# Gate and up products of a feed-forward as 2x2 block products: seven quarter products instead of eight

## The chip, the cores and the metric

The kernel runs on one core of one Trainium2 chip. The metric is the device time of one execution, in microseconds. Three runs of the kernel before took 3021.64 to 3022.8 us, median 3022.2. The engines are called TensorE (PE in the profile's rows), VectorE (DVE), ScalarE (ACT), GpSimd (POOL) and SyncE (SP), whose queue here starts the loads of weights.

## What is computed

Two encoder layers over 512 tokens of width 1024, all in float32. Cut to its skeleton, the reference is:

```python
def swiglu(x, w_gate, w_up, w_down):
    return (jax.nn.silu(x @ w_gate) * (x @ w_up)) @ w_down
...
for i in range(DEPTH):
    h = h + 0.5 * swiglu(rms_norm(h, ffn1_norm[i]), ffn1_w_gate[i], ffn1_w_up[i], ffn1_w_down[i])
    u = rms_norm(h, mix_norm[i])
    proj = u @ w_in[i]
    ...
    h = h + merged @ w_out[i]
    h = h + 0.5 * swiglu(rms_norm(h, ffn2_norm[i]), ffn2_w_gate[i], ffn2_w_up[i], ffn2_w_down[i])
    gate = jax.nn.sigmoid(rms_norm(h, ple_norm[i]) @ ple_w_gate[i])
    h = h + gate * (p[i] @ ple_w_proj[i])
return rms_norm(h, final_norm)
```

`w_gate` and `w_up` are 1024 x 2816, `w_down` is 2816 x 1024. `merged` is the gated sum of three attentions, which the change does not touch.

## The kernel before, in words

**Layout.** The stream `h` lies on chip as eight tiles of 128 features x 512 tokens. A product computes 128 output features x 512 tokens in one PSUM bank. To keep float32 accuracy, each operand is split into a rounded high part and the rest (`hi`, `lo`), and every product is three matmuls: high by high, low by high, high by low (`mm3`, whose matmuls the profile gives as L165). One column tile of gate or up takes 8 x 3 = 24 matmuls of 512 columns.

**Weights.** All weights come as 456 chunks of 128 x 1024 (512 KB), in the order of use, through SyncE's queue (`Weights.load`, four buffers `wraw`). `Weights.halve` splits a chunk: ScalarE casts the high part (L75), VectorE subtracts for the low part (L76; in the mixes GpSimd does that, by `lo_engine`). `get` keeps the splits two chunks ahead of the products and the loads five.

**Feed-forward** (`ffn`, called for FFN1 and FFN2 of each layer, `ffn10`, `ffn20`, `ffn11`, `ffn21` in the profile). Its right operand `z` (named `f_0z`, `f_1z`) is h times the norm's gain, split, made per tile of h by `Prep.split` (ScalarE L328, VectorE L329) while the stage before ends; the reciprocal root of the mean square is multiplied in later, and the squares are added up on GpSimd (L287). For each of 22 column tiles `f`: gate, up, then VectorE multiplies both by the root (L386, L388), ScalarE applies Silu (L387), VectorE multiplies (L389) and the result is split (L175, L176). After the tiles of a group (2, 4, 4, 4, 4, 4) its down products follow, whose sums VectorE adds to h (L371).

**Around it.** A mix ends with the output projection (`w_out`, `add_out`): the first four tiles of h are summed while the last attention heads still run; the other four come after them, all four at once, chunk after chunk over the rows. Then VectorE adds each sum to h (L944) and calls the preparation for FFN2. `ple` multiplies in the layer embedding: per tile a gate product, a tanh on ScalarE, three operations on VectorE (L972, L974, L975), then the preparation of the next layer's FFN1.

**Order.** Each engine runs its queue in order. A scheduler places the instructions by their priority in the program and by what they wait for; the order on record of each engine is what is compared below. `S` gives one of `SLOTS` = 79 buffers of 128 x 512; `PS` gives one of eight PSUM banks.

Of the kernel before, what the change touches and what calls it, by code (L numbers as in the profile page):

```python
# [45 lines left out]
class Weights:  # L46
# [21 lines left out]
    def halve(self, upto):  # L68
        while self.split < min(upto, self.total):
            n = self.split  # L70
            self.load(n + 1)
            raw = self.raw.pop(n)
            hi = self.pool.tile([P, 1024], F32R, tag="whi", name=f"whi{n}", bufs=3)
            lo = self.pool.tile([P, 1024], F32R, tag="wlo", name=f"wlo{n}", bufs=3)
            self.nc.scalar.copy(hi, raw)  # L75
            self.lo_engine.tensor_tensor(lo, raw, hi.bitcast(F32), op=ALU.subtract)  # L76
# [60 lines left out]
def encoder_kernel(ctx: ExitStack, tc: tile.TileContext, ins, out):  # L137
# [8 lines left out]
    W = Weights(nc, wpool, ins["wall"])  # L146

# [206 lines left out]
    def ffn(l, tag, prep, after, hooks={}):  # L354
        name = f"{tag}{l}"
        z = prep.z
        a = {}
        rb = None

        def down(g, final=False):  # L360
            fs = GROUPS[g]
# [13 lines left out]
        for f in range(FT):
            pg, pu = PS(f"{name}g{f}"), PS(f"{name}u{f}")
            gate, up = ("cols", tag + "_w_gate", l, f), ("cols", tag + "_w_up", l, f)
            if f == 0:
                together((pg, pu), W.get(gate, up), z)
                rb, emit = prep.norm.rstd()  # L380
                emit()
            else:
                run(proj(pg, W.get(gate), z))
                run(proj(pu, W.get(up), z))
            g1, u1 = S(f"{name}g1_{f}"), S(f"{name}u1_{f}")
            nc.vector.tensor_mul(g1, pg, rb)  # L386
            nc.scalar.activation(g1, g1, AF.Silu)  # L387
            nc.vector.tensor_mul(u1, pu, rb)  # L388
            nc.vector.tensor_mul(u1, u1, g1)  # L389
            a[f] = split(u1, f"{name}a{f}")  # L390
            for g, fs in enumerate(GROUPS[:-2]):
                if f == fs[-1] + 1:
                    down(g)
            if f in hooks:
                hooks[f]()
        root_table()
        down(len(GROUPS) - 2)
# [782 lines left out]
```

## Time and profile before

| | |
|---|---|
| median of three runs | 3022.2 us |
| the profiled execution | 3021.5 us |
| its span in the trace | 3019.7 us |
| first FFN1 / its mix / its FFN2 (us from the span's start) | 9.7 to 375.5 / 375.5 to 1103.2 / 1103.2 to 1463.1 |
| layer embedding, layer 0 | 1463.1 to 1507.5 |
| second FFN1 / its mix / its FFN2 | 1507.5 to 1868.5 / 1868.5 to 2598.2 / 2598.2 to 2958.2 |
| VectorE in a FFN2 of 360 us | 184 us busy |
| GpSimd in a FFN2 of 360 us | 15 us busy |

A row of the timeline gives the start, the duration, the engine, the line, the operation, its tile and operands, its shape, and in brackets the idle time before it and who ended it. A recorded duration holds some overlap with the next instruction, so the step from start to start is the price in a full queue.

### The profile page before, as it was taken

What the parts mean: (1) busy time and instruction counts of PE and PEld (TensorE: products, weight loads), DVE (VectorE), ACT (ScalarE), POOL (GpSimd) and SP (SyncE); (2) the same over time, 40 slices, a digit from 0 to 9 for tenths busy, and PEclk for the clock granted to TensorE, in tenths of its full rate; (3) what the DMA queues carried; (4) which work ended last, traced back from release to release, by engine and by line L of the source; (5) the groups of instructions that cost most, each with busy time, mean ns of one, the idle gap of its engine ahead of it and who ended that gap; (6) DMA issues with size and microseconds to landing.
All of it is one profiled execution on the core that took longest, in us unless ns stands there. A gap on an engine that the chain in (4) does not pass through costs nothing.

```text
span 3019.7 us, 37502 instructions
## 1 busy us (share of the span) xinstructions
PE 2966.6 (98%) x14206; PEld 2463.6 (82%) x14206; DVE 1837.0 (61%) x2844; ACT 1418.5 (47%) x2511; POOL 749.0 (25%) x709
## 2 busy tenths in 40 slices
PE   8999999999999999999999999999999999999998
PEld 7888878888878888888888888788888788888886
DVE  6444576646787765444664445866478877644446
ACT  4222356655677742223432223566467777422233
POOL 0010015444455530000200001144344555200003
PEclk9999999999999999999999999999999999999999
DMA  4363332122222233333333334211222222333332
GB/s 154 99 221 98 122 126 70 49 70 73 77 77 79 76 116 98 97 93 97 125 103 95 96 98 158 83 63 57 63 82 74 68 75 75 124 95 96 98 98 91
DMA packets 81525, 287.75 MB, mean 95 GB/s; under 512 B 10382, under 2 KB 12430, under 8 KB 81344
## 3 DMA queue, kind: packets, MB, share of 16 engines
q1 hardware_dynamic: 66960, 240.42, 25.5%
q0 software_dynamic: 12080, 42.00, 4.1%
q10 hardware_dynamic: 2304, 2.94, 0.3%
q8 instruction: 111, 1.82, 0.2%
q14 instruction: 70, 0.57, 0.1%
HBM read 274.76 MB, written 18.94 MB: 97 GB/s over the span
## 4 chain that ended last, share of the span: by engine, by line
PE 88%; DVE 6%; ACT 4%; issue 2%; POOL 0%; DMA 0%; ACTq 0%; DVEq 0%; POOLq 0%
PE ffn10g L165 4%; PE ffn10u L165 4%; PE ffn21g L165 4%; PE ffn20g L165 4%; PE ffn21u L165 4%; PE ffn20u L165 4%; PE ffn21d L165 4%; PE ffn11d L165 4%; PE ffn10d L165 4%; PE ffn20d L165 4%; PE ffn11g L165 4%; PE ffn11u L165 4%; PE wo L165 3%; PE ple L165 3%; PE m1ga L165 1%
## 5 line engine op out<-in xcount | busy, mean ns | idle before, releaser
L75 ACT CAST whi<-wraw 128x1024 fp32r<-128x1024 f32 x456 | 478.4, 1052 | 1057.0 <-issue 371.3
L76 DVE TENSOR_TENSOR wlo<-wraw,whi 128x1024 fp32r<-128x1024 f32 x312 | 383.6, 1232 | 124.3 <-ACT whi L75 124.0
L76 POOL TENSOR_TENSOR wlo<-wraw,whi 128x1024 fp32r<-128x1024 f32 x144 | 353.4, 2457 | 366.5 <-ACT whi L75 322.0
L287 POOL TENSOR_TENSOR pg0sq<-pg0sq,pg0sq 128x512 f32<-128x512 f32 x7 | 11.1, 1586 | 345.0 <-ACT pg0sq L282 345.0
L287 POOL TENSOR_TENSOR pg1sq<-pg1sq,pg1sq 128x512 f32<-128x512 f32 x7 | 11.1, 1583 | 345.1 <-ACT pg1sq L282 345.1
L419 POOL DMA_DIRECT2D h_dram<-wo0h x8 | 4.3, 541 | 341.2 <-DVE wo0h L371 341.2
L371 DVE SCALAR_TENSOR_TENSOR wo0h<-ffn11d,wo0h 128x512 f32<-128x512 f32 x48 | 32.8, 689 | 40.9 <-PE ffn11d L165 40.9
L371 DVE SCALAR_TENSOR_TENSOR x<-ffn10d,x 128x512 f32<-128x512 f32 x48 | 32.8, 689 | 40.9 <-PE ffn10d L165 40.9
L371 DVE SCALAR_TENSOR_TENSOR wo1h<-ffn21d,wo1h 128x512 f32<-128x512 f32 x48 | 32.8, 689 | 38.7 <-PE ffn21d L165 38.7
L371 DVE SCALAR_TENSOR_TENSOR wo0h<-ffn20d,wo0h 128x512 f32<-128x512 f32 x48 | 32.8, 689 | 38.7 <-PE ffn20d L165 38.7
L388 DVE TENSOR_TENSOR ffn20u<-ffn20u,f_0r 128x512 f32<-128x512 f32 x22 | 15.2, 691 | 62.0 <-PE ffn20u L165 62.0
L388 DVE TENSOR_TENSOR ffn21u<-ffn21u,f_1r 128x512 f32<-128x512 f32 x22 | 15.2, 691 | 62.0 <-PE ffn21u L165 62.0
L388 DVE TENSOR_TENSOR ffn10u<-ffn10u,f_0r 128x512 f32<-128x512 f32 x22 | 15.2, 691 | 59.8 <-PE ffn10u L165 59.8
L419 POOL DMA_DIRECT2D h_dram<-x x8 | 4.3, 540 | 189.1 <-DVE x L371 189.1
L388 DVE TENSOR_TENSOR ffn11u<-ffn11u,f_1r 128x512 f32<-128x512 f32 x22 | 15.2, 691 | 59.2 <-PE ffn11u L165 59.2
L386 DVE TENSOR_TENSOR ffn21g<-ffn21g,f_1r 128x512 f32<-128x512 f32 x22 | 15.2, 691 | 47.0 <-PE ffn21g L165 46.9
L386 DVE TENSOR_TENSOR ffn20g<-ffn20g,f_0r 128x512 f32<-128x512 f32 x22 | 15.2, 691 | 47.0 <-PE ffn20g L165 46.9
L386 DVE TENSOR_TENSOR ffn10g<-ffn10g,f_0r 128x512 f32<-128x512 f32 x22 | 15.2, 691 | 44.5 <-PE ffn10g L165 44.4
L386 DVE TENSOR_TENSOR ffn11g<-ffn11g,f_1r 128x512 f32<-128x512 f32 x22 | 15.2, 690 | 44.1 <-PE ffn11g L165 44.1
L248 POOL DMA_DIRECT2D bias_s<-bvs x1 | 0.5, 519 | 142.5 <-DVE bvs L246 142.5
L287 POOL TENSOR_TENSOR f_1sq<-f_1sq,f_1sq 128x512 f32<-128x512 f32 x14 | 21.0, 1500 | 58.5 <-ACT f_1sq L282 58.3
L598 ACT CAST m0kc<-m0kc 64x512 fp32r<-64x512 f32 x32 | 18.6, 580 | 13.7 <-PE m0kc L165 6.1
(5072 smaller groups left out, 10383.7 us busy)
## 6 DMA issues: line engine op xcount, KB each, us to landing
wraw<-in_wall SPq DMA_DIRECT2D x456, 512.0 KB, 3.5
copies_s<-bias_s POOLq DMA_DIRECT2D x16, 256.0 KB, 7.7
copies_d<-bias_d POOLq DMA_DIRECT2D x8, 512.0 KB, 15.1
h_dram<-x POOLq DMA_DIRECT2D x8, 256.0 KB, 2.7
pp_dram<-m0ppt POOLq DMA_DIRECT2D x8, 256.0 KB, 4.7
wo0h<-h_dram POOLq DMA_DIRECT2D x8, 256.0 KB, 5.3
ple0p<-pp_dram POOLq DMA_DIRECT2D x8, 256.0 KB, 4.9
h_dram<-wo0h POOLq DMA_DIRECT2D x8, 256.0 KB, 2.7
```

The lines of the kernel that those rows point to most:

```text
L75: self.nc.scalar.copy(hi, raw)
L76: self.lo_engine.tensor_tensor(lo, raw, hi.bitcast(F32), op=ALU.subtract)
L165: nc.tensor.matmul(ps, lhsT, rhs, start=start, stop=stop, skip_group_check=True)
L248: nc.gpsimd.dma_start(bias_s, bv[0:n, :])
L287: self.engine.tensor_tensor(self.acc, self.acc, sq, op=ALU.add)
L371: nc.vector.scalar_tensor_tensor(h[d], ps, 0.5, h[d], op0=ALU.mult, op1=ALU.add)
L386: nc.vector.tensor_mul(g1, pg, rb)
L388: nc.vector.tensor_mul(u1, pu, rb)
L419: nc.gpsimd.dma_start(h_dram[d], h[d])
L598: nc.scalar.copy(ks[e][r], ps[own])
```

## The change

Gate and up are computed for pairs of column tiles. The chunks of the two tiles are called `X` and `Y`; the left half of each holds the tile's first 512 rows, the right half the other 512. The 512 tokens are cut into halves `A` and `B` of 256. So a pair is a product of 2x2 blocks, for which Winograd's form of Strassen's scheme needs seven block products, four additions of weights, four of right operands and seven of results, instead of eight products. A block product is 4 x 3 = 12 matmuls of 256 columns (line L228 now), and a pair of tiles takes 84 of these instead of 48 of 512. There are 86 such blocks; layer 0's first pair of FFN1 is computed as before (`plain_pair`). In the order on record, matmuls of 512 columns go from 11334 to 7206, of 256 from 1458 to 8682; two-tensor operations of 512 on VectorE from 733 to 1179 and on GpSimd from 67 to 497.

The sums of weights stand on GpSimd (`Quad.add`), the additions of results on ScalarE (copies), VectorE and, one of them, GpSimd. The weights are split by halves of a chunk. The right operands come from `Combos` in place of `Prep`:

```diff
+        def operands(self, d):
+            name, k, gain = self.name, d % 4, col(self.l, self.at + d)
+            A, B = HALVES
+            if d < 4:
+                zf = S(f"{name}zf{d}")
+                nc.scalar.activation(zf, h[d], AF.Copy, scale=gain)
...
+                hi, lo = [t[:, HALVES[d % 2]] for t in self.both]
+                nc.scalar.copy(hi, zf[:, A])
+                nc.vector.tensor_sub(lo, zf[:, A], hi.bitcast(F32))
+                self.pair(1, k, hi, lo)
+                t = S(f"{name}t13{k}")
+                nc.vector.tensor_sub(t[:, A], zf[:, B], zf[:, A])
+                th, tl = S(f"{name}t13{k}h", F32R), S(f"{name}t13{k}l", F32R)
+                nc.scalar.copy(th[:, A], t[:, A])
+                nc.vector.tensor_sub(tl[:, A], t[:, A], th[:, A].bitcast(F32))
+                self.pair(5, k, th[:, A], tl[:, A])
...
+            else:
+                zf, t, th, tl = self.first[k]
...
+                nc.scalar.activation(hi, h[d], AF.Copy, scale=gain)
+                w = S(f"{name}t24{k}")
+                nc.vector.scalar_tensor_tensor(w[:, A], h[d][:, B], gain, t[:, A], op0=ALU.mult, op1=ALU.subtract)
+                nc.vector.scalar_tensor_tensor(w[:, B], h[d][:, A], gain, w[:, A], op0=ALU.mult, op1=ALU.subtract)
+                nc.vector.scalar_tensor_tensor(t[:, B], h[d][:, B], gain, zf[:, B], op0=ALU.mult, op1=ALU.subtract)
+                nc.vector.scalar_tensor_tensor(lo, h[d], gain, hi.bitcast(F32), op0=ALU.mult, op1=ALU.subtract)
...
+                nc.scalar.copy(wh, w)
+                nc.vector.tensor_sub(wl, w, wh.bitcast(F32))
...
+                nc.scalar.copy(th[:, B], t[:, B])
+                nc.vector.tensor_sub(tl[:, B], t[:, B], th[:, B].bitcast(F32))
...
+    class Quad:
+        def add(self):
+            X, Y = [W.raw[n] for n in self.places]
...
+            nc.gpsimd.tensor_tensor(s12[:, L], Y[:, L], Y[:, R], op=ALU.add)
+            nc.gpsimd.tensor_tensor(s12[:, R], s12[:, L], X[:, L], op=ALU.subtract)
+            nc.gpsimd.tensor_tensor(s34[:, L], X[:, L], Y[:, L], op=ALU.subtract)
+            nc.gpsimd.tensor_tensor(s34[:, R], X[:, R], s12[:, R], op=ALU.subtract)
+            self.source = {1: X[:, L], 2: X[:, R], 4: Y[:, R], 5: s12[:, L], 6: s12[:, R], 7: s34[:, L], 3: s34[:, R]}
...
+            if i == 1:
+                nc.scalar.copy(t1[:, A], self.R)
+            elif i == 5:
+                nc.scalar.copy(t2[:, A], self.Q)
+            elif i == 2:
+                nc.vector.tensor_add(t1[:, A], self.V, t1[:, A])
+            elif i == 6:
+                nc.scalar.copy(t1[:, B], self.R)
+            elif i == 3:
+                nc.vector.tensor_add(t1[:, B], self.Q, t1[:, B])
+            elif i == 7:
+                nc.scalar.copy(t2[:, B], self.R)
+                nc.gpsimd.tensor_tensor(t2[:, B], t2[:, A], t2[:, B], op=ALU.add)
...
+        def gate_half(q, n):
+            t, r = q.t[n], rb[0]
+            if n == 0:
+                nc.vector.tensor_mul(t, t, r)
             else:
...
+                nc.gpsimd.tensor_tensor(t[:, B], t[:, B], r[:, B], op=ALU.mult)
+                nc.vector.tensor_mul(t[:, A], q.R, r[:, A])
+            nc.scalar.activation(t, t, AF.Silu)
+            nc.gpsimd.tensor_tensor(t, t, r, op=ALU.mult)
+
+        def up_half(q, gq, n, f):
+            t, g = q.t[n], gq.t[n]
+            if n == 0:
+                nc.vector.tensor_mul(t, t, g)
+            else:
+                nc.vector.tensor_mul(t[:, A], q.R, g[:, A])
+                nc.vector.tensor_mul(t[:, B], t[:, B], g[:, B])
+            a[f] = split(t, f"{name}a{f}")
```

The products of a pair stand in the order G1 G5, U1 U5, G2 U2, G6 U6, G3 U3, G7 U7 (G is gate, U is up); product 4 of both follows after the next pair's G5. The down groups follow pairs 1, 3, 5, 7 and the last. Splits run two whole split tiles ahead of the products (`AHEAD`), the sums of weights six steps ahead of the splits. Buffers: 62 instead of 79 slots, and a stage's pool in their place, which holds 4 more raw chunks, a fourth split tile and the sums in a feed-forward, and 17 kept tiles in a mix. In the output projection the second half is now done one tile of h after another (24 matmuls each):

```diff
         def piece(half, kk):
+            if half == 1:
+                d = 4 + kk
+                sums[d] = PS(f"{name}{d}")
+                yield from proj(sums[d], W.get(("cols", "w_out", l, d)), m)
+                return
...
         for d in range(KT):
-            if d == 4:
-                for gen in outs:
-                    run(gen)
+            if d >= 4:
+                run(outs[d - 4])
```

**The start of FFN2 of layer 0, in the engines' own order.** First TensorE, where the output projection's last matmuls (`wo`) end and the stage begins. Before:

```order
L165 MATMUL ffn20g_10132<-f_0z0h,whi_10040 128x512
L165 MATMUL ffn20g_10132<-f_0z0h,wlo_10041 128x512
L165 MATMUL ffn20g_10132<-f_0z0l,whi_10040 128x512
```

and the change:

```order
L228 MATMUL wo_11538<-m0mg7l,whi_11445 128x512
L228 MATMUL ffn20g0R<-f_0b110h,whi_11595 128x256
L228 MATMUL ffn20g0R<-f_0b110h,wlo_11596 128x256
L228 MATMUL ffn20g0R<-f_0b110l,whi_11595 128x256
L228 MATMUL ffn20g0R<-f_0b110h,whi_11595 128x256
```

The matmuls are half as wide and take a half of a split tile (`whi`, `wlo`) each.

VectorE at the same place, where tile 4 and 5 of h are added in (`wo0h`). Before, one operation per tile makes the low part of its right operand (L329), beside whole chunks (L76):

```order
L944 SCALAR_TENSOR_TENSOR wo0h_9937<-wo_9982,wo0h_9937 128x512
L944 SCALAR_TENSOR_TENSOR wo0h_9939<-wo_9986,wo0h_9939 128x512
L944 SCALAR_TENSOR_TENSOR wo0h_9941<-wo_9990,wo0h_9941 128x512
L329 SCALAR_TENSOR_TENSOR f_0z4l<-wo0h_9937,small,f_0z4h 128x512
L944 SCALAR_TENSOR_TENSOR wo0h_9943<-wo_9994,wo0h_9943 128x512
L329 SCALAR_TENSOR_TENSOR f_0z5l<-wo0h_9939,small,f_0z5h 128x512
```

In the change (`f_0t` are the differences of right operands, `f_0b2` and `f_0t240l` the low parts of operands 2 and 3, 6 and 4; `ffn20g0s` a sum of weights):

```order
L1271 SCALAR_TENSOR_TENSOR wo0h_11330<-wo_11444,wo0h_11330 128x512
L449 TENSOR_TENSOR f_0t_11386<-f_0zf_11382 128x256
L464 SCALAR_TENSOR_TENSOR f_0t_11356<-wo0h_11330,small,f_0zf_11352 128x256
L445 TENSOR_TENSOR f_0b112l<-f_0zf_11382,f_0b112h 128x256
L452 TENSOR_TENSOR f_0t133l<-f_0t_11386,f_0t133h 128x256
L111 TENSOR_TENSOR wlo_11596<-wraw_11290,whi_11595 128x512
L461 SCALAR_TENSOR_TENSOR f_0t_11430<-wo0h_11328,small,f_0t_11343 128x256
L111 TENSOR_TENSOR wlo_11596<-ffn20g0s_11583,whi_11595 128x512
L462 SCALAR_TENSOR_TENSOR f_0t_11430<-wo0h_11328,small,f_0t_11430 128x256
L465 SCALAR_TENSOR_TENSOR f_0b20l<-wo0h_11328,small,f_0b20h 128x512
L474 TENSOR_TENSOR f_0t131l<-f_0t_11356,f_0t131h 128x256
L470 TENSOR_TENSOR f_0t240l<-f_0t_11430,f_0t240h 128x512
```

Five operations for one tile of h, and split halves of a chunk and of a sum, now stand between two additions to h.

GpSimd at the same place. Before, the loads of h and then the sums of squares:

```order
L938 DMA wo0h_9941<-h_dram 128x512
L938 DMA wo0h_9943<-h_dram 128x512
L287 TENSOR_TENSOR f_0sq_9950<-f_0sq_9950,f_0sq_9957 128x512
L287 TENSOR_TENSOR f_0sq_9950<-f_0sq_9950,f_0sq_9965 128x512
L287 TENSOR_TENSOR f_0sq_9950<-f_0sq_9950,f_0sq_9973 128x512
```

In the change:

```order
L1266 DMA wo0h_11334<-h_dram 128x512
L489 TENSOR_TENSOR ffn20g0s_11583<-wraw_11400 128x512
L491 TENSOR_TENSOR ffn20g0s_11584<-wraw_11290,wraw_11400 128x512
L490 TENSOR_TENSOR ffn20g0s_11583<-ffn20g0s_11583,wraw_11290 128x512
L489 TENSOR_TENSOR ffn20u0s_11589<-wraw_11494 128x512
L492 TENSOR_TENSOR ffn20g0s_11584<-wraw_11290,ffn20g0s_11583 128x512
L490 TENSOR_TENSOR ffn20u0s_11589<-ffn20u0s_11589,wraw_11449 128x512
L491 TENSOR_TENSOR ffn20u0s_11590<-wraw_11449,wraw_11494 128x512
L492 TENSOR_TENSOR ffn20u0s_11590<-wraw_11449,ffn20u0s_11589 128x512
L351 TENSOR_TENSOR f_0sq_11349<-f_0sq_11349,f_0sq_11362 128x512
```

Eight sums of weights of the first pair's gate and up stand ahead of the first sum of squares.

More of the change, by code (lines that the diff above doesn't have):

```diff
@@ L66, in load, with tiles, part, halve @@
             self.loaded += 1
-    def halve(self, upto):
+    def tiles(self, stage=None):
+        n = self.pairs
+        self.pairs += 1
+        if stage is not None and n % 4 == 3:
+            return tuple(stage.tile([P, 1024], F32R, tag=f"w{x}2", name=f"w{x}{n}", bufs=1) for x in ("hi", "lo"))
+        return tuple(self.pool.tile([P, 1024], F32R, tag=f"w{x}", name=f"w{x}{n}", bufs=3) for x in ("hi", "lo"))
+    def part(self, hi, lo, raw):
+        self.nc.scalar.copy(hi, raw)
+        self.lo_engine.tensor_tensor(lo, raw, hi.bitcast(F32), op=ALU.subtract)
+    def halve(self, upto, stage=None):
         while self.split < min(upto, self.total):
             n = self.split
+            if whole(n):
+                self.split += 1
+                continue
             self.load(n + 1)
[L72 to L76, printed above, removed]
+            hi, lo = self.tiles(stage)
+            self.part(hi, lo, self.raw.pop(n))
             self.parts[n] = (hi, lo)
             self.split += 1
-    def get(self, *keys):
+    def claim(self, *keys):
         first = len(self.keys)
@@ L375, in ffn @@
[L375 to L381, printed above, removed]
-            else:
[L383 to L395, printed above, removed]
@@ L397, in ffn @@
+        at = len(steps)
         down(len(GROUPS) - 2)
+        for k, fn in enumerate(tail):
+            fn()
+            steps.insert(at + 2 + k, steps.pop())
         down(len(GROUPS) - 1, True)
+        if plain:
+            plain_pair()
+        quads = []
+        for kind, what, _ in steps:
+            if kind == "product" and what[0] not in quads:
+                quads.append(what[0])
+        order = []
+        for kind, what, _ in steps:
+            if kind == "down":
+                order.append(("down", what))
+            elif what[0].places is None:
+                q = what[0]
+                q.places = ()
+                order.append(("quad", q))
@@ new lines, in ffn, with sums_upto @@
+        for kind, what in order:
+            if kind == "down":
+                W.claim(what)
+            else:
+                what.places = W.claim(*[("cols", what.w, l, 2 * what.p + e) for e in range(2)])
+        base = {}
+        for kind, what in order:
+            base[id(what) if kind == "quad" else what] = what.places[0] if kind == "quad" else W.keys.index(what)
+        ready, state = {}, {"n": 0, "half": None, "tiles": 0, "sums": 0}
+        def sums_upto(n):
+            while state["sums"] < min(n, len(steps)):
+                kind, what, _ = steps[state["sums"]]
+                if kind == "product" and what[0].sums is None:
+                    W.load(what[0].places[-1] + 1)
+                    what[0].add()
+                state["sums"] += 1
```

255 lines of the change are left out of this document (221 added, 34 removed).

## The prediction, as it was put on record before the run

> **What bounds the kernel now.** I read the profile's head first, then the chain of work that ended last, then the engines' busy time by stage, and only then single stretches of the timeline. From the page:
>
> ```profile
> span 3019.7 us, 37502 instructions
> PE 2966.6 (98%) x14206; PEld 2463.6 (82%) x14206; DVE 1837.0 (61%) x2844; ACT 1418.5 (47%) x2511; POOL 749.0 (25%) x709
> ...
> PE 88%; DVE 6%; ACT 4%; issue 2%; POOL 0%; DMA 0%; ACTq 0%; DVEq 0%; POOLq 0%
> ```
>
> TensorE is busy for 98% of the span and carries 88% of the chain. The busy time by stage (first feed-forward, mix, second feed-forward of layer 0; then both feed-forwards of layer 1; the columns are the stretch, its length, and each engine's busy time) says where others matter:
>
> ```profile
> 9.70:375.50 365.80, 365.80 (x1592) 299.87 (x1593) 192.07 (x242) 117.44 (x144) 20.02 (x38) 1.00 0.41 135
> 375.50:1103.20 727.70, 714.35 (x3721) 598.20 (x3720) 508.60 (x929) 461.70 (x951) 328.10 (x295) 1.00 0.26 81
> 1103.20:1463.10 359.90, 359.90 (x1587) 297.68 (x1586) 184.37 (x215) 111.51 (x136) 15.10 (x10) 1.00 0.31 97
> ...
> 1507.50:1868.50 361.00, 360.64 (x1587) 297.44 (x1587) 185.38 (x223) 110.21 (x133) 10.02 (x13) 1.00 0.32 102
> ...
> 2598.20:2958.20 360.00, 360.00 (x1588) 297.72 (x1587) 184.39 (x215) 111.52 (x136) 15.16 (x10) 1.00 0.31 97
> ```
>
> In a feed-forward TensorE never waits: 359.90 of 359.90 us. VectorE works half the time, ScalarE a third, GpSimd 4%. So fewer columns through TensorE are saved one for one, until what is added to VectorE and GpSimd makes TensorE wait. That is the whole question.
>
> **The change, part by part: what TensorE saves.** Two stretches of TensorE's timeline, first and last row of each, the granted clock being 1.00 in all:
>
> ```profile
> 97.67 0.39 PE L165 MATMUL ffn10u<-f_0z3l,whi 128*128 128x512 f32 x1
> ...
> 101.52 0.39 PE L165 MATMUL ffn10d<-ffn10a3h,wlo 128*128 128x512 f32 x1
> ```
>
> ```profile
> 2997.23 0.28 PE L165 MATMUL ple<-pg1z0h,wlo 128*128 128x256 f32 x1
> ...
> 2999.63 0.28 PE L165 MATMUL ple<-pg1z7h,whi 128*128 128x256 f32 x1
> ```
>
> Seventeen steps in 3.85 us are 226.5 ns per 512-column matmul; twenty steps in 2.40 us are 120.0 ns per 256-column one, that is 7 ns more than half. A block pair of two column tiles took 48 matmuls of 512 and takes 84 of 256: 10.87 us become 10.08, only 7% instead of an eighth. There are 86 such blocks (gate and up, 11 pairs, four feed-forwards, less the plainly computed first pair of the first one): 4128 x 0.2265 - 7224 x 0.1200 = 935.0 - 866.9 = **68 us saved**, some 17 per feed-forward. [...]
>
> The down products, the mixes and the gates of the layer embedding keep their matmuls. The second half of the output projection is only computed one tile after another, and the chunk loads stay 456:
>
> ```profile
> wraw<-in_wall SPq DMA_DIRECT2D x456, 512.0 KB, 3.5
> ```
>
> Four chunks per pair of tiles at 3.5 us each, in eight buffers instead of four, against 20 us of products: I cost the loads at nothing, hidden behind the products; without that cover a late chunk costs its 3.5 us at a stage's start.
>
> **What is added on VectorE and GpSimd.** Prices, from the timelines of VectorE (start to start) and from groups:
>
> ```profile
> 465.20 0.68 DVE L531 TENSOR_TENSOR m0qa<-m0qa,m0trig 128x512 f32<-128x512 f32 x1
> 465.80 0.67 DVE L539 TENSOR_TENSOR m0ka20l<-m0kap,m0ka20h 64x512 fp32r<-64x512 f32 x1
> ...
> 1084.71 1.22 DVE L76 TENSOR_TENSOR wlo<-wraw,whi 128x1024 fp32r<-128x1024 f32 x1
> 1085.84 1.78 DVE L329 SCALAR_TENSOR_TENSOR f_0z0l<-wo0h,small,f_0z0h 128x512 fp32r<-128x512 f32 x1
> 1087.55 1.78 DVE L329 SCALAR_TENSOR_TENSOR f_0z1l<-wo0h,small,f_0z1h 128x512 fp32r<-128x512 f32 x1
> 1089.25 1.77 DVE L329 SCALAR_TENSOR_TENSOR f_0z2l<-wo0h,small,f_0z2h 128x512 fp32r<-128x512 f32 x1
> 1090.95 0.74 DVE L329 SCALAR_TENSOR_TENSOR f_0z3l<-wo0h,small,f_0z3h 128x512 fp32r<-128x512 f32 x1
> 1091.61 1.21 DVE L76 TENSOR_TENSOR wlo<-wraw,whi 128x1024 fp32r<-128x1024 f32 x1
> ```
>
> ```profile
> L619 DVE TENSOR_TENSOR m0vc<-m0vc,m0vc x16: 361/420/426, 620.5 to 839.3; 128x256 fp32r<-128x256 f32 x16
> ```
>
> ```profile
> 1085.10 5.37 POOL L287 TENSOR_TENSOR f_0sq<-f_0sq,f_0sq 128x512 f32<-128x512 f32 x3 [2.71 <-ACT f_0sq L282]
> ```
>
> Alone, VectorE takes 0.60 us for a two-tensor operation of 512, 1.13 for 1024, 0.66 for one with a scalar, and, taking 0.09 of overlap off the recorded 0.42, 0.33 for 256 (0.40 with a scalar). But in the three rows from 1085.84 it takes 1.70 a step while GpSimd adds: each GpSimd addition of 512 costs VectorE 1.70 - 0.66 = **1.04 us**. An operation with an input in PSUM escapes that; `m0A11t` lies there, and three such operations take 0.63 each inside a pair of GpSimd's (632.16 to 636.91):
>
> ```profile
> 632.16 4.75 POOL L76 TENSOR_TENSOR wlo<-wraw,whi 128x1024 fp32r<-128x1024 f32 x2
> ```
>
> ```profile
> 635.31 1.89 DVE L640 TENSOR_TENSOR m0A11ptl<-m0A11t,m0A11pth 128x512 fp32r<-128x512 f32 x3 [0.31 <-ACT m0A11pth L639]
> ```
>
> In the steady part, two tile pairs and one down group are 4 x 84 x 0.1200 + 96 x 0.2265 = 62.1 us of TensorE. VectorE has there 36 two-tensor operations of 512 (28 of them halves of weight splits), 14 of 256, 4 of 1024 and 8 additions to h: 21.6 + 4.6 + 4.5 + 5.3 = 36.0 us. GpSimd has 20 operations of 512 (16 sums of weights, 4 products) and 6 of 256: with 1.04 and half of it, 20.8 + 3.1 = 23.9 us. Together 59.9 of 62.1 if every one falls on a busy VectorE. About 9 us of VectorE's work reads PSUM and is not held, so it is nearer 57. It fits, barely, and splits run two tiles ahead, so I take 8 us for all four feed-forwards, between 0 and the rival's 88. ScalarE's 28 half casts, 4 whole ones, 4 activations and some 20 smaller copies are 35 us at most by these rows, hidden behind the 62 (without that cover TensorE would wait for the first cast, 0.6 us):
>
> ```profile
> L75 ACT CAST whi<-wraw 128x1024 fp32r<-128x1024 f32 x456 | 478.4, 1052 | 1057.0 <-issue 371.3 <-PE ffn10d L165 75.4 <-PE ffn11d L165 75.3
> ...
> L598 ACT CAST m0kc<-m0kc 64x512 fp32r<-64x512 f32 x32 | 18.6, 580 | 13.7 <-PE m0kc L165 6.1 <-DVE m0kc7l L600 1.7 <-DVE m0kc1l L600 1.6
> ```
>
> **The four starts** are where I see the gain go. The seven right operands are formed by VectorE per 128 rows of h: from h[4] on it has 3 operations of 256 with a scalar, one of 512, and two splits for each, where one stood before. TensorE wants the third product (operand 2) four products of 1.44 us, 5.8 us, after the stage begins.
>
> *Second feed-forwards.* From the first h addition of the output projection to the split for operand 2, VectorE's queue has 51 rows: 12 x 0.66 + 12 x 0.40 + 15 x 0.33 + 10 x 0.60 + 2 x 1.13 = 26 us. TensorE offers 96 x 0.2265 + 5.8 = 27.5 us. So nothing is lost without GpSimd; but 8 sums of weights and up to 7 sums of squares stand there, 15 x 1.04 = 15.6 us, and it is late by 14. A split that waits in the same queue for its chunk adds a landing or two: bounds 0 and 20. I take 10 each, since the 8 additions to h read PSUM and a sum that runs while VectorE waits costs nothing.
>
> *Feed-forward 1, layer 1.* VectorE begins after the reciprocal of the layer embedding; TensorE's stage begins at 1507.5:
>
> ```profile
> 1476.93 3.35 DVE L309 RECIPROCAL pg0r<-pg0r 128x512 f32<-128x512 f32 x1
> 1480.32 0.69 DVE L972 TENSOR_TENSOR ple0t<-ple,pg0r 128x512 f32<-128x512 f32 x1
> ```
>
> 72 rows, 39.4 us by the same prices, end at 1519.7; operand 2 is wanted at 1507.5 + 5.8 = 1513.3. Late by 6 without GpSimd, 22 with its 15 additions. I take 15.
>
> *Feed-forward 1, layer 0.* The operands are formed behind the reciprocal, when tile 0 is done:
>
> ```profile
> 27.83 3.35 DVE L309 RECIPROCAL f_0r<-f_0r 128x512 f32<-128x512 f32 x1 [1.29 <-ACT f_0r L308]
> 31.22 0.69 DVE L386 TENSOR_TENSOR ffn10g<-ffn10g,f_0r 128x512 f32<-128x512 f32 x1
> ...
> 40.98 0.69 DVE L386 TENSOR_TENSOR ffn10g<-ffn10g,f_0r 128x512 f32<-128x512 f32 x1 [1.04 <-PE ffn10g L165]
> ```
>
> Tile 2's gate ended at 40.98, so it began 24 x 0.2265 = 5.4 earlier, at 35.5: there the first block begins, and operand 2 is wanted at 41.3. VectorE's 46 rows from 31.2 are 21.4 us and end at 52.6: late by 11 alone, by 20 with eight additions of GpSimd. I take 15.
>
> **The sum**, against the profiled execution of 3021.5 us (span 3019.7; the median shown is 3022.2, 0.7 more): -68 + 10 + 10 + 15 + 15 + 8 = **-10**, so 3011.5, and 3012 against the median. The parts change only how late the starts are: 17 to 82 us, and the steady part.
>
> **Rivals.** *The starts are covered.* If the weight sums run before VectorE is busy, only the 6 and 11 us that VectorE alone needs remain: -68 + 17 = -51, 2971. For it: GpSimd is idle in all feed-forwards before (15 of 360 us). Against it: the sums wait for chunks, whose buffers come free late.
>
> *VectorE is the bound all through the feed-forwards, and the kernel slower.* Place: the weight splits and GpSimd's sums; price: what one GpSimd operation takes from VectorE. It decides from (62.1 - 36.0 - 3.1) / 20 = 1.15 us, and 1.04 is measured. A lone GpSimd addition lasts 1.29:
>
> ```profile
> L848 POOL TENSOR_TENSOR m0mg<-m0mg,m0C2r x1: 1290/1290/1290, 842.6 to 842.6; 128x512 f32<-128x512 f32 x1
> ```
>
> If VectorE loses that whole time, 36.0 + 20 x 1.29 + 6 x 0.65 = 65.7, 3.6 us over in each of 21.5 such periods, 77 in all, and nothing is made up after a late start: 3012 - 8 + 77 = 3081. For it: the three rows above, and how little room is left. Against it: the PSUM operands. [...]
>
> *The saving is not what the counts say.* If a 256-column matmul in the new stream costs half of a 512-column one (113 ns), 50 us more are saved: 2962; the twenty steps above speak against it.
>
> **How the numbers follow.** Forecast 0.48 (own range 2990 to 3042), starts covered 0.25, VectorE bound 0.25, cheaper matmuls 0.02. The range that leaves out the ends of the two outer cases is 2966 to 3078. About 0.2% (6 us) is what a measurement can tell from no change. Faster by more: 0.27 from two rivals and half of the forecast's, 0.50; within: 0.12; slower: 0.13 of the forecast's and the 0.25, 0.38.
>
> **What would show it.** In the changed profile: TensorE's busy time lower by some 68 us; steps of 120 ns in the blocks; TensorE's waits at the four starts, released by VectorE's splits, of 10 to 15 us each; few waits later in a feed-forward; VectorE's half splits at 1.6 us or more beside GpSimd's sums. It is wrong if the steps are not 120 ns, if waits stand all through the feed-forwards (VectorE bound), or if the starts show under 20 us together.

## The result, and the profile after

The changed kernel takes 3169.0 us (median of 4 runs, 3168.08 to 3169.99) against 3022.3 us before: a ratio of 1.0486, 95% interval [1.0467, 1.0504]. It is 147 us slower, where 10 us faster was forecast, and outside the range of 2966 to 3078.

The page's head and the chain that ended last, of the changed kernel:

```profile
span 3166.3 us, 46195 instructions
...
PE 2966.7 (94%) x17302; PEld 2597.3 (82%) x17302; DVE 2302.0 (73%) x3523; ACT 1701.5 (54%) x3359; POOL 1509.1 (48%) x1268
...
PE 47%; DVE 18%; issue 14%; POOL 12%; ACT 7%; DMA 3%; ACTq 0%; DVEq 0%; POOLq 0%
```

TensorE's share of the chain fell from 88% to 47%. Its busy time is 2966.7 us as before (2966.6), though gate and up should take 7% less of its time; that odd equality is the first thing to explain. Busy time by stage, for the same stages as before (the column behind the engines is the granted clock):

```profile
10.20:423.40 413.20, 372.78 (x2313) 335.63 (x2314) 308.85 (x409) 190.62 (x351) 199.23 (x173) 0.94 0.35 118
423.40:1156.60 733.20, 717.49 (x3721) 598.93 (x3720) 512.66 (x942) 464.76 (x961) 338.26 (x303) 1.00 0.25 81
1156.60:1544.70 388.10, 357.27 (x2380) 331.28 (x2379) 294.22 (x372) 177.82 (x338) 198.64 (x146) 0.95 0.28 93
...
1589.10:1989.60 400.50, 358.75 (x2380) 330.89 (x2379) 306.52 (x393) 181.68 (x346) 196.65 (x152) 0.94 0.28 92
1989.60:2723.50 733.90, 717.16 (x3722) 598.77 (x3721) 513.16 (x942) 464.35 (x961) 335.98 (x300) 1.00 0.25 81
2723.50:3104.70 381.20, 352.30 (x2379) 327.22 (x2378) 292.77 (x374) 178.75 (x340) 200.11 (x146) 0.96 0.27 89
```

The four feed-forwards take 1583.0 us instead of 1446.7 (136 more), the two mixes 1467.1 instead of 1457.4 (10 more). The granted clock, 1.00 in all stages before, is 0.94 to 0.96 in the feed-forwards alone. VectorE is busy for 294 of 388 us in the FFN2 of layer 0 and so is not the bound all through it. Of the 10 us of the mixes, a part is one wait in each output projection for a weight split (2.97 us before 1149.65, 3.54 before 2716.69); the rest was not traced.

What TensorE waited for in that FFN2 (engine, tile and line, then who released it; total, times, longest):

```profile
PE ffn20u0R L228 <- DVE wlo L111: 7.1, 1, 7.1
PE ffn20d L228 <- DVE wo0h L556: 7.0, 1, 7.0
PE f_0ss L371 <- POOL f_0sq L351: 4.3, 1, 4.3
PE ffn20u9R L228 <- ACT ffn20u9t L515: 4.0, 1, 4.0
PE ffn20g0V L228 <- DVE wlo L111: 1.6, 1, 1.6
PE ffn20g6R L228 <- ACT ffn20g6t L525: 1.2, 1, 1.2
```

Four kinds: splits and operands at the start, the norm's total (`f_0ss`), the first down group (`ffn20d`), and single waits later (4.0 us in pair 9 of the pairs 0 to 10, and 1.2 us in pairs 2, 4, 6 and 8). Adding up, over all matmuls of the four feed-forwards in the trace, what the step to the next one exceeds the full-speed step (120 or 226.7 ns) gives 166 us in steps with a wait and 46 us in steps without one. The second sum is the clock: the 335 steps that start while half clock is recorded, and have no idle gap above 0.15 us behind them, are 45.9 us over in all. (How the 212 us divide depends on what counts as a wait: by idle gaps above 0.15 us, the profile's own bar, it is 151 and 61.) It is seen right behind the 7.0 us wait at the first down group, in TensorE's timeline:

```profile
1221.47 0.39 PE L228 MATMUL ffn20d<-ffn20a1l,whi 128*128 128x512 f32 x1
1228.87 0.77 PE L228 MATMUL ffn20d<-ffn20a0h,whi 128*128 128x512 f32 x1 [7.01 <-DVE wo0h L556]
1229.43 0.63 PE L228 MATMUL ffn20d<-ffn20a0h,wlo 128*128 128x512 f32 x1
1229.86 0.63 PE L228 MATMUL ffn20d<-ffn20a0l,whi 128*128 128x512 f32 x1
...
1234.55 0.61 PE L228 MATMUL ffn20d<-ffn20a0h,wlo 128*128 128x512 f32 x1
1234.98 0.42 PE L228 MATMUL ffn20d<-ffn20a0l,whi 128*128 128x512 f32 x1
1235.23 0.40 PE L228 MATMUL ffn20d<-ffn20a1h,whi 128*128 128x512 f32 x1
```

Steps are 427 ns instead of 227 for 6 us, so the wait of 7.0 us costs some 3 us more. Such slow matmuls count as busy (0.63 us recorded instead of 0.39), which is how the busy time stayed equal: 68 us of matmul time went, and slow steps and the longer tails of a matmul that nothing follows (0.39 us at 1221.47, where a step is 0.23) came.

The balance: -68 (gate and up) + 166 - 2 (waits now and before) + 46 - 5 (slow steps now and before) + 10 (mixes) = +147 us, as measured.

### The profile page after: what moved, and what is told of

Read it like the earlier page. It is cut to its first block, busy times and chain, and to the rows that moved or that the text cites. A ratio compares the mean times of both kernels' runs of the same rounds, so it can differ in the third digit from the quotient of the medians.

```text
span 3166.3 us, 46195 instructions
## 1 busy us (share of the span) xinstructions
PE 2966.7 (94%) x17302; PEld 2597.3 (82%) x17302; DVE 2302.0 (73%) x3523; ACT 1701.5 (54%) x3359; POOL 1509.1 (48%) x1268
## 4 chain that ended last, share of the span: by engine, by line
PE 47%; DVE 18%; issue 14%; POOL 12%; ACT 7%; DMA 3%; ACTq 0%; DVEq 0%; POOLq 0%
DVE wlo L111 6%; DMA wraw<-in_wall 2%; PE ple L228 2%; PE ffn10d L228 2%; PE m0ga L228 1%; ACT whi L110 1%; PE m1ga L228 1%; PE ffn21d L228 1%; PE ffn11d L228 1%; PE ffn20d L228 1%; PE m0gb L228 1%; PE m1gb L228 1%; PE m0vc L228 1%; PE m1vc L228 1%; PE wo L228 1%
## 5 line engine op out<-in xcount | busy, mean ns | idle before, releaser
L110 ACT CAST whi<-wraw 128x1024 fp32r<-128x1024 f32 (+1 forms) x542 | 449.9, 847 | 424.2 <-issue 108.5
L111 DVE TENSOR_TENSOR wlo<-wraw,whi 128x512 fp32r<-128x512 f32 (+1 forms) x398 | 413.4, 1054 | 64.5 <-ACT whi L110 63.8
L556 DVE SCALAR_TENSOR_TENSOR wo0h<-ffn11d,wo0h 128x512 f32<-128x512 f32 x48 | 32.5, 686 | 28.2 <-PE ffn11d L228 28.2
L556 DVE SCALAR_TENSOR_TENSOR wo0h<-ffn20d,wo0h 128x512 f32<-128x512 f32 x48 | 32.5, 686 | 26.0 <-PE ffn20d L228 25.9
L556 DVE SCALAR_TENSOR_TENSOR wo1h<-ffn21d,wo1h 128x512 f32<-128x512 f32 x48 | 32.3, 685 | 24.3 <-PE ffn21d L228 24.3
L556 DVE SCALAR_TENSOR_TENSOR x<-ffn10d,x 128x512 f32<-128x512 f32 x48 | 32.1, 684 | 20.4 <-PE ffn10d L228 20.4
L919 ACT CAST m1kc<-m1kc 64x512 fp32r<-64x512 f32 x32 | 18.6, 581 | 17.3 <-PE m1kc L228 14.0
L872 DVE SCALAR_TENSOR_TENSOR m1qc<-m1qc,m1qc 64x512 fp32r<-64x512 f32 x16 | 11.0, 688 | 20.0 <-ACT m1qc L871 19.9
L872 DVE SCALAR_TENSOR_TENSOR m0qc<-m0qc,m0qc 64x512 fp32r<-64x512 f32 x16 | 11.0, 688 | 20.0 <-ACT m0qc L871 19.9
L1338 POOL TENSOR_SCALAR out<-wo1h,small 128x512 f32<-128x512 f32 (+1 forms) x9 | 7.2, 799 | 32.1 <-DVE wo1h L1302 29.4
L871 ACT ACTIVATE m1qc<-m1qc 64x512 fp32r<-64x512 f32 x16 | 9.5, 592 | 22.7 <-PE m1qc L228 13.2
L871 ACT ACTIVATE m0qc<-m0qc 64x512 fp32r<-64x512 f32 x16 | 9.5, 592 | 21.5 <-PE m0qc L228 13.2
L351 POOL TENSOR_TENSOR f_0sq<-f_0sq,f_0sq 128x512 f32<-128x512 f32 x7 | 13.2, 1893 | 14.6 <-ACT f_0sq L346 14.6
```

Source lines behind the costliest of these rows:

```text
L351: self.engine.tensor_tensor(self.acc, self.acc, sq, op=ALU.add)
L871: nc.scalar.activation(qs[e][own], ps[own], AF.Copy, scale=-0.125)
L872: nc.vector.scalar_tensor_tensor(qs[e][other], ps[own], -0.125, qs[e][own].bitcast(F32), op0=ALU.mult, op1=ALU.subtract)
L919: nc.scalar.copy(ks[e][r], ps[own])
L1338: nc.gpsimd.tensor_scalar(gained[d][:, c], h[d][:, c], small[:, L * S_N + d:L * S_N + d + 1], 1.0, op0=ALU.mult, op1=ALU.mult)
```

## The experiments

Eleven kernels ran, once each, but for the one with the operands spread, which ran four times; the kernel before beside them took 3022.0 to 3022.6 us (medians). The waits and slow steps given are of the four feed-forwards, added up as above (166 and 46 in the change). Where waits are given by place, every step more than 0.2 us over is counted, which takes in a few slow steps: in the change 70 us at the starts, 20 for the norm's total, 26 at the first down groups and 57 later, 173 in all. Two theories are held against each other first. *GpSimd*: the loss is what its sums take from VectorE (1.04 us each by the rows in the prediction) and what stands behind them in its own queue. *VectorE*: it has too much to do at the starts, whoever adds.

**Sums on VectorE.**

```diff
-            nc.gpsimd.tensor_tensor(s12[:, L], Y[:, L], Y[:, R], op=ALU.add)
+            nc.vector.tensor_tensor(s12[:, L], Y[:, L], Y[:, R], op=ALU.add)
...
```

> The four sums of weights of each block stand on VectorE instead of GpSimd; nothing else is changed. [...] Theory VectorE (VectorE has too much to do at the starts whoever adds): its queue gets 0.6 us longer per sum, waits stay at 166 or more, 3170 to 3200 us.

Measured: 3076.5 us, 92 less than the change. Waits 100, slow steps 29. VectorE takes four more operations per block and everything gets earlier, so theory VectorE falls, with its 3170 us and waits of 166 or more. VectorE's load hardly moves: in the FFN2 of layer 0 it is busy 297 us with 455 operations, against 294 with 372. What GpSimd's sums do to VectorE is seen in the changed kernel at the start of FFN2, VectorE's timeline first, then GpSimd's:

```profile
1155.54 0.68 DVE L111 TENSOR_TENSOR wlo<-ffn20g0s,whi 128x512 fp32r<-128x512 f32 x1
1156.14 1.51 DVE L462 SCALAR_TENSOR_TENSOR f_0t<-wo0h,small,f_0t 128x256 f32<-128x256 f32 x1
1157.57 1.78 DVE L465 SCALAR_TENSOR_TENSOR f_0b20l<-wo0h,small,f_0b20h 128x512 fp32r<-128x512 f32 x1
1159.27 1.49 DVE L474 TENSOR_TENSOR f_0t131l<-f_0t,f_0t131h 128x256 fp32r<-128x256 f32 x1
1160.69 1.74 DVE L470 TENSOR_TENSOR f_0t240l<-f_0t,f_0t240h 128x512 fp32r<-128x512 f32 x1
1162.36 0.47 DVE L461 SCALAR_TENSOR_TENSOR f_0t<-wo0h,small,f_0t 128x256 f32<-128x256 f32 x1
```

```profile
1157.33 1.47 POOL L489 TENSOR_TENSOR ffn20g1s<-wraw 128x512 f32<-128x512 f32 x1
1158.88 1.60 POOL L490 TENSOR_TENSOR ffn20g1s<-ffn20g1s,wraw 128x512 f32<-128x512 f32 x1
1160.45 1.44 POOL L351 TENSOR_TENSOR f_0sq<-f_0sq,f_0sq 128x512 f32<-128x512 f32 x1
```

While GpSimd adds, the two take turns in these rows, one start of VectorE after each of GpSimd (1157.33 and 1157.57, 1158.88 and 1159.27, 1160.45 and 1160.69): an operation of 256 that takes 0.47 us at 1162.36 takes 1.5, one of 512 takes 1.75. From start to start they take 1.43 and 1.70 us instead of 0.40 and 0.66: the toll is about 1.04 us per turn, for 256 as for 512; the price in the prediction was right.

**Sums left out.**

> The sums of weights are left out: products 5, 6, 7 and 3 take a raw quarter instead of a sum. All matmuls, splits, right operands and result additions remain. Theory GpSimd: waits under 70 us, about 3030 us. Theory VectorE: the starts keep their waits, only those for GpSimd's sums of squares and for the product with the root go, 3100 to 3130 us.

Measured: 3038.2 us, waits 74, slow steps 19. Nearly the first theory (3030). Two things in it bear on the prediction. Of the waits, 53 us are at the starts, where the operands are formed, though no sum of weights is left there; and 12 of the 20 us for the norm's total are left, at both FFN2 as much as before (5.4 and 4.2 us). VectorE's busy time in the FFN2 of layer 0 falls from 294.2 to 246.8 us, with as many operations: the 80 sums in that stretch cost it 0.59 us each on average, as much as doing them itself (0.60).

**Operand differences left out.**

> The differences of right operands are left out: all seven operands are halves of the plain split tiles, one operation on ScalarE and one on VectorE per tile of h, as before the change. The sums of weights stay on GpSimd. Theory VectorE: the waits at the starts go almost entirely (some 100 us with the half clock behind them), about 3060 us. Theory GpSimd: the starts still wait for sums and sums of squares, the first down group and the ninth pair wait as they did, 3110 to 3140 us.

Measured: 3118.4 us, waits 126, slow steps 35. The second theory: the waits for operands and splits at the starts fall from 70 to 25 us; those for the norm's total (22), at the first down group (27) and later (57) stay within 2 us. Leaving out the operands gains 51 us, leaving out the sums 131; the two overlap, and together exceed the 147 us.

**Seven waits put into the kernel before.**

```diff
+    def pause(name, f, src):
+        t = S(f"{name}pause{f}")
+        nc.vector.tensor_copy(t, src)
+        for _ in range(DELAYS[f]):
+            nc.gpsimd.tensor_scalar(t, t, 1.0, 1.0, op0=ALU.mult, op1=ALU.mult)
+        ps = PS(f"{name}pause{f}")
+        tc.keep_in_program_order(nc.tensor.matmul(ps, ones, t, start=True, stop=True))
...
+DELAYS = {4: 2, 7: 4, 9: 7, 12: 12, 15: 8, 17: 14, 20: 18}
```

> The kernel before, with seven waits put into FFN2 of layer 0: ahead of tiles 4, 7, 9, 12, 15, 17, 20 one matmul waits for a chain of 2, 4, 7, 12, 8, 14, 18 GpSimd operations that starts when the tile before is done (some 2 to 17 us, less what TensorE does meanwhile). Theory clock: behind a wait of more than some 4 us the 512-column matmuls take 427 ns instead of 227 for some 6 us, behind shorter ones they do not; each longer wait costs some 3 us more than itself. Rival: the slow steps in the changed kernel come from its 256-column stream, and here a wait costs itself alone.

Measured: 3052.9 us. In three places TensorE had enough other work and hardly waited; four waits remained, of 2.1, 3.1, 4.0 and 7.4 us. TensorE's timeline around the second and the third:

```profile
1305.37 0.39 PE L165 MATMUL ffn20u<-f_0z7h,whi 128*128 128x512 f32 x1
1308.85 1.12 PE L409 MATMUL ffn20pause<-ffn20pause,ones 128*128 128x512 f32 x2 [3.10 <-POOL ffn20pause L407]
1309.41 0.80 PE L165 MATMUL ffn20u<-f_0z7h,wlo 128*128 128x512 f32 x1
1310.05 0.39 PE L165 MATMUL ffn20u<-f_0z7l,whi 128*128 128x512 f32 x1
```

```profile
1392.15 1.75 PE L409 MATMUL ffn20pause<-ffn20pause,ones 128*128 128x512 f32 x2 [3.96 <-POOL ffn20pause L407]
1392.91 1.41 PE L165 MATMUL ffn20g<-f_0z0h,whi 128*128 128x512 f32 x1
1394.12 0.63 PE L165 MATMUL ffn20g<-f_0z0h,wlo 128*128 128x512 f32 x1
1394.55 0.63 PE L165 MATMUL ffn20g<-f_0z0l,whi 128*128 128x512 f32 x1
...
1396.12 0.39 PE L165 MATMUL ffn20g<-f_0z2h,whi 128*128 128x512 f32 x1
```

Behind 3.1 us the slow step is not seen: but for the first one behind the pause (0.64 us, as also 0.63 behind the wait of 2.1 us), the matmuls are recorded with 0.39 us, as ahead of the wait. Behind 4.0 us the step is 0.43 for 4.0 us, and behind 7.4 us for 6.0 (1434.33 to 1440.4). So the theory of the clock holds, in a kernel without a single block product: a long wait costs more than itself, by some 2 and 3 us here (half of the 4.0 and 6.0).

A sharp line between 3.1 and 4.0 us does not follow from four waits, and the other traces show that there is none. In all thirteen traces (both kernels and the eleven runs), take TensorE's waits before 3000 us that stand alone, with no other wait above 0.3 us in the 10 us before and the 5 us after. Of 132 such waits of 0.8 to 1.9 us none is followed by half clock, of 36 between 1.9 and 3.4 us 25 are, and all 48 longer ones are. Behind these the half clock lasts a whole multiple of 3.41 us in the record (3.41, 6.83 or 10.24 us in the change), often begun during the wait (2.9 us into the 7.0 us before 1228.87); of the half-clock time that lies behind the wait, half is lost, 1.5 to 3.2 us. One stretch of 3.4 us in this run (from 146.7 us) stands behind no wait at all, but behind six matmuls of 33 rows; in the kernel before, the same six (from 144.23 us) have full clock behind them. What else sets the clock is not shown.

**Only what others wait for is taken off GpSimd.**

```diff
-                nc.gpsimd.tensor_tensor(t2[:, B], t2[:, A], t2[:, B], op=ALU.add)
+                nc.vector.tensor_tensor(t2[:, B], t2[:, A], t2[:, B], op=ALU.add)
...
-            nc.gpsimd.tensor_tensor(t, t, r, op=ALU.mult)
+            nc.vector.tensor_tensor(t, t, r, op=ALU.mult)
...
-            self.norm = Norm(name, D, nc.gpsimd)
+            self.norm = Norm(name, D, nc.vector)
```

> The sums of weights stay on GpSimd, but what others wait for is taken off its queue: the product with the root, the last addition of results (of gate and up) and the sums of squares in the feed-forwards stand on VectorE. Theory queue (most of the loss is work that stands in GpSimd's queue behind sums that wait for their chunks): the waits at the first down group (24 us), in the ninth pair (17 us) and for the sum of squares (17 us) go, and the half clock behind them: about 3090 us. Theory port (the loss is VectorE being held by the sums): the waits for VectorE's splits stay, VectorE has more to do: 3140 us or more.

Measured: 3104.2 us, 65 less, waits 113, slow steps 33. Between the two theories and nearer to the queue (of the second, what the runs show is that the sums hold VectorE, 1.04 us per turn; a port as the cause is not shown): later waits fall from 57 to 22 us, those for the norm's total from 20 to 12, those at the starts only from 70 to 65, at the first down group from 26 to 22. VectorE's load is not what fell: in the FFN2 of layer 0 it is busy 311 us, against 294 in the change. How the queue held TensorE is seen in the change in pair 9, in the order of time:

```profile
1459.94 1.30 POOL L489 TENSOR_TENSOR ffn20g10s<-wraw 128x512 f32<-128x512 f32 x1 [2.43 <-DVE wlo L111]
...
1464.60 1.26 POOL L590 TENSOR_TENSOR ffn20g8t<-ffn20g8t,f_0r 128x512 f32<-128x512 f32 x1
1465.89 0.42 DVE L597 TENSOR_TENSOR ffn20u8t<-ffn20u8R,ffn20g8t 128x256 f32<-128x256 f32 x1 [2.40 <-POOL ffn20g8t L590]
1467.39 0.62 ACT L239 CAST ffn20a17h<-ffn20u8t 128x512 fp32r<-128x512 f32 x1 [5.44 <-DVE ffn20u8t L598]
1467.92 0.36 ACT L515 COPY ffn20u9t<-ffn20u9R 128x256 f32<-128x256 f32 x1
1468.34 0.58 PE L228 MATMUL ffn20u9R<-f_0t240h,whi 128*128 128x256 f32 x1 [4.04 <-ACT ffn20u9t L515]
```

Three sums of pair 10, begun when a split of VectorE released them, stand ahead of pair 8's product with the root (L590); VectorE's L597 waits for that product, ScalarE's cast for VectorE, the copy out of PSUM stands behind the cast, and TensorE waits 4.0 us for the copy. With the product taken off GpSimd, 0.4 us of this wait is left, though 2.2 us come up later in the same pair. At the first down group the same happens in the change, GpSimd's timeline, then VectorE's:

```profile
1215.03 1.30 POOL L489 TENSOR_TENSOR ffn20g2s<-wraw 128x512 f32<-128x512 f32 x1 [10.01 <-DMA wraw<-in_wall]
1216.29 1.30 POOL L491 TENSOR_TENSOR ffn20g2s<-wraw,wraw 128x512 f32<-128x512 f32 x1
...
1220.49 1.29 POOL L492 TENSOR_TENSOR ffn20g2s<-wraw,ffn20g2s 128x512 f32<-128x512 f32 x1
1221.74 1.26 POOL L590 TENSOR_TENSOR ffn20g1t<-ffn20g1t,f_0r 128x512 f32<-128x512 f32 x1
```

```profile
1217.01 1.12 DVE L111 TENSOR_TENSOR wlo<-ffn20g2s,whi 128x512 fp32r<-128x512 f32 x1 [1.84 <-ACT whi L110]
1223.04 1.73 DVE L595 TENSOR_TENSOR ffn20u1t<-ffn20u1t,ffn20g1t 128x512 f32<-128x512 f32 x1 [4.90 <-POOL ffn20g1t L590]
1224.69 1.75 DVE L111 TENSOR_TENSOR wlo<-wraw,whi 128x512 fp32r<-128x512 f32 x1
1226.37 1.75 DVE L240 TENSOR_TENSOR ffn20a2l<-ffn20u1t,ffn20a2h 128x512 fp32r<-128x512 f32 x1
1228.05 1.28 DVE L556 SCALAR_TENSOR_TENSOR wo0h<-ffn20d,wo0h 128x512 f32<-128x512 f32 x2
```

GpSimd idles 10 us for a chunk that the second pair's sums need; then the product with the root (L590) of the pair before stands behind five of them; VectorE's L595 waits for it and holds the additions to h (L556) behind it, so no PSUM bank comes free and TensorE waits 7.0 us. The chunk is late for a reason of its own: its load was issued at 1210.68, when a split of VectorE released the buffer, and landed 4.3 us later.

Here the order in GpSimd's queue is only the smaller part, though. With the product off the queue, TensorE still waits 4.8 of the 7.0 us: the eight sums now run in one piece, from 1186.37 to 1199.5 us, and each operation of VectorE ahead of the additions to h takes 1.5 to 1.8 us beside them. GpSimd is idle nearly half of the stage in the change, so it is not overloaded; what hurts is what stands behind a sum, and that the sums come together.

**All of a block's work on VectorE**, the norm's total later (the edits of the first run, the first two pairs of lines of the last one, and):

```diff
-                product(q, 5, rstd if q is U and p == 0 else lambda: None)
+                product(q, 5)
...
-                product(G, i, (lambda G=G: gate_half(G, 0)) if i == 3 else lambda: None)
+                product(G, i, (lambda G=G: gate_half(G, 0)) if i == 3 else rstd if i == 6 and p == 0 else lambda: None)
```

> As the run with the sums on VectorE, and also the product with the root and the last addition of results on VectorE, and the norm's total is multiplied after product 6 of the first gate instead of after product 5 of the first up. Theory queue: of the 100 us of waits left there, those at the down groups (25 us) and for the norm's total (12 us) go: about 3045 us. Theory VectorE: its queue is longer by 20 operations of 512 per two pairs than in the changed kernel, and it becomes late all through: over 3076 us.

Measured: 3033.3 us, waits 69, slow steps 21; the first theory, and 12 us better than it said; the waits after the starts are gone (1 us later on, 5 at the first down group). The stage of layer 0's FFN2:

```profile
1112.10:1469.30 357.20, 348.31 (x2380) 325.61 (x2379) 302.78 (x510) 181.25 (x338) 17.53 (x11) 0.98 0.30 101
```

VectorE is busy for 303 of 357 us, with 138 more operations than in the change, and is late nowhere but at the starts, where 64 us are left.

**Plain pairs at the starts**, with all of a block's work on VectorE: one pair as layer 0's FFN1 has it, then two, then two with the operands spread.

```diff
-        for p in range(1 if plain else 0, PAIRS):
+        for p in range(NP, PAIRS):
...
-        ffn(l, "ffn1", prep, pm, hooks, plain if l == 0 else None)
+        ffn(l, "ffn1", prep, pm, hooks, plain)
```

> All of a block's work on VectorE, and the first pair of tiles of every feed-forward is computed plainly, as layer 0's first one is; the right operands are formed meanwhile. It gives up 3 x 2 blocks (5 us of the 68). Theory starts: the waits at the starts of the other three feed-forwards go: 3010 to 3025 us. Rival: VectorE makes 16 more operations there (the plain operand too) and is as late, 3045 us or more.

Measured: 3044.8 us, waits 67, slow steps 26. The rival: one plain pair is no cure.

> The same with two plain pairs at every start: 7 x 2 blocks or 11 us of the 68 given up against the change, and 44 us of TensorE's time to form the operands. Theory starts: hardly any wait is left, 2985 to 3005 us. Rival (VectorE's load in the steady part decides): no better than one plain pair, 3020 us or more.

Measured: 3001.5 us, waits 23, slow steps 13: the first theory. The starts fall from 55 to 3 us, 21 are left at the first down group.

```diff
-                if f == 0:
-                    for d in range(KT):
-                        prep.operands(d)
+                for d in range(2 * f, 2 * f + 2):
+                    prep.operands(d)
```

> Two plain pairs at every start, all of a block's work on VectorE, and the right operands of two tiles of h are formed behind each of the four plain tiles instead of all eight behind the first. Theory starts: what is left of the waits (5 us in front of the first down group in both FFN1, whose h additions stand in VectorE's queue behind the operands) goes: 2980 to 2995 us. Rival: the operands come late for the first blocks instead: 3000 us or more.

Measured: 2998.1 us (median of 4 runs, 2995.9 to 2998.4), a ratio of 0.9918, interval [0.9902, 0.9935], against the kernel before: 24 us or 0.8% faster than it, with all four runs below all seven of the kernel before, and 171 us below the change. Neither estimate holds: the spreading gains some 3 us, against a single run without it. Waits 18, slow steps 10. Of its stages:

```profile
1102.20:1450.30 348.10, 346.92 (x2236) 317.26 (x2235) 285.81 (x481) 175.14 (x317) 9.52 (x7) 1.00 0.31 102
...
2588.10:2934.90 346.80, 346.49 (x2236) 317.17 (x2236) 286.44 (x481) 175.48 (x317) 10.00 (x7) 1.00 0.29 96
```

The clock is 1.00 again, and the FFN2 take 347 to 348 us instead of 360: 57 us of matmul time should be saved in all four feed-forwards, and 38 of them are (1409.0 against 1446.7). The mixes take 14 us more than before; why was not tried: their waits are small and many, and moved with the order.

**Two plain pairs, with GpSimd as in the change, and with the sums alone on it.**

> Two plain pairs at every start, but the engines as in the change: sums, last additions and products with the root on GpSimd. Against the 3001.5 us with all of these on VectorE this shows what GpSimd costs apart from the starts. Theory GpSimd: pair 9 (17 us) and the 1.4 us behind every second pair (20 us) stay, with the half clock some 45 us: about 3050 us. Theory starts (GpSimd matters only while the operands are formed): 3015 us or less.

Measured: 3094.7 us, waits 100, slow steps 29: later waits 51, first down group 49, starts 3. The first theory, and 45 us worse than it said.

> The same with only the sums on GpSimd; the last additions and products with the root on VectorE. Theory port (VectorE loses 1.04 us to each sum, 60 of 62 us are full): waits all through the feed-forwards, 3040 us or more. Theory queue (what hurt was standing behind the sums in GpSimd's queue): VectorE catches up, 3000 to 3015 us.

Measured: 3060.4 us, waits 69, slow steps 21: later waits 19, first down group still 49. Neither estimate quite, and the first nearer. With 3001.5 us for the same with a block's work all on VectorE: the product with the root and the last additions in GpSimd's queue cost 34 us, the sums themselves 59. The first down group shows how the sums cost time with nothing behind them in their queue: in the FFN2 of layer 0 eight of them run from 1151.90 to 1164.86 us beside the forming of the operands, 8 x 1.04 = 8.3 us by the toll, and TensorE waits 8.9 us there instead of 2.2.

## Why the prediction was wrong

**The saving: right.** 68 us were forecast. The steps in the blocks are 120 ns wherever TensorE neither waits nor is slow, and taking waits and slow steps off the result gives the 68.

**The price of GpSimd on VectorE: right, but used in the wrong sum.** 1.04 us per turn was measured again. The prediction added VectorE's and GpSimd's time, found 59.9 of 62.1 us, and wrote "It fits, barely, and splits run two tiles ahead, so I take 8 us". By load it does fit: VectorE is busy 294 of 388 us in the stage, and with all of a block's work on it 303 of 357. This is the step that failed: the steady part was judged by load alone and priced at 8 us. Behind the starts, TensorE waited 83 us (26 at the first down groups, 57 later), and half clock came on top.

The runs showed two things in its place. The first is a chain through queues: a sum that waits, for a chunk or for a split of VectorE, stands ahead of the product with the root on GpSimd; behind that product stand the additions to h on VectorE or the copies out of PSUM on ScalarE, and behind these TensorE. Taking that product, the last additions and the sums of squares off GpSimd was worth 65 us with the sums still there, and 34 us (without the sums of squares) where the starts were covered. The second is the sums themselves, which come in bursts and then hold VectorE for the length of the burst (1.5 to 1.8 us recorded per operation beside the burst of 1186.37 to 1199.5 us above); they cost another 59 us where the starts were covered, though on average they take no more of VectorE's time on GpSimd (0.59 us each) than on VectorE (0.60). How the 59 us divide between VectorE's turns and the sums' own waits was not separated.

**The starts: right place, too small, and the wrong reason.** 50 us were forecast; measured are 70 for splits and operands and 20 for the norm's total. By stage, the first kind: 13 (forecast 15) in layer 0's FFN1, 31 (15) in layer 1's, 13 and 13 (10 each) in the FFN2. Only the FFN1 of layer 1 was far off, outside its bound of 22. That the other three come near is luck. The prediction put the lateness of the FFN2 down to GpSimd's sums ("nothing is lost without GpSimd") and gave the four starts 17 us without them. With the sums left out they still wait 53 us (9 and 13 at the FFN2), and with the operand differences left out 25. It summed VectorE's work up to operand 2; but at the FFN2 of layer 0 TensorE waits first, for 7.1 us, for the weight split of its third product (`ffn20u0R`), whose low part VectorE reaches at 1166.81, behind operations for operands that are wanted later.

The norm's total was no term at all. Its sums of squares stand in GpSimd's queue with the sums of weights, but that these delay it is shown for layer 0's FFN1 alone, where its wait falls from 10.0 to 1.6 us without them. At the FFN2 of layer 0 the squares themselves come late: GpSimd waits 10.8 us for them.

**The clock: a term that was missing.** It took 46 us, since half clock followed every lone wait of TensorE above 3.4 us (48 of 48), and 25 of 36 between 1.9 and 3.4. In the feed-forwards of the profile before nothing showed it, as TensorE hardly waited there; only the end of the kernel did, where the clock is 0.50 behind a wait of 2.37 us (from 3006 us on). A sum with waits of 50 us should have carried it as an unknown.

**ScalarE and the loads at nothing: half right.** ScalarE's time fits (178 of 388 us), but its copies out of PSUM were late in the queue behind casts that wait for VectorE (the 4.0 us in each pair 9). The loads land in 3.5 us as before, but they are issued late, when VectorE's splits release their buffers: one sum waited 10 us for a chunk, and work that others need stood behind it.

**The rivals.** "VectorE is the bound" named 3081 us, by a load that does not fit; the load does fit, but it was right that waits stand all through the feed-forwards. (The "rival's 88" in the steady part's range is 77 in the rival's own sum.) "The starts are covered" fell. The range was too narrow because both ends of the steady part were worked out from load.

## What to carry to other kernels

Work that is moved to an idle engine should be judged by what stands behind it in that engine's queue and by what its own inputs wait for, and only then by its time; here 16 additions per period (two tile pairs and a down group) on an engine that was 4% busy cost more than the same additions on one that was half busy. In these traces every lone wait of TensorE above 3.4 us (48 of 48), and 25 of 36 between 1.9 and 3.4, had half clock behind it, which cost another 1.5 to 3.2 us: a sum that forecasts such waits should carry it as a term. A scheme that saves columns needs its operands ready at the stage's start: two plain tile pairs, 11 us of the saving, bought back nearly all of the starts (64 us of waits became 3), though 21 us were left at the first down group.

## What the hardware showed unexpectedly

Where both engines had a full queue and neither of VectorE's two operands lay in PSUM, VectorE and GpSimd took turns operation by operation (from 1157.33 us in the change): the toll of 1.04 us was the same for 256 and for 512, so short operations suffered most (0.47 us became 1.5, where one of 512 went from 0.74 to 1.78). A lone wait of TensorE was followed by half clock in 25 of 36 cases between 1.9 and 3.4 us, and in all 48 above. And a 256-column matmul took 120 ns at full clock and 213 ns at half (from 1463.29 and 1468.72 us in the change), as a 512-column one took 227 and 427 (from 1220.79 and 1229.43).
